# Tables in 128 rows of 1 KB, spread by TensorE into PSUM, in a rotary-embedding kernel

## Chip, cores and metric

The kernel runs on one core of a Trainium2 chip. The metric is the device time of one execution in microseconds (us), median of several executions. The profile's span, from the first instruction to the last, is 1.8 us shorter than that time in the kernel before. All runs compared here are in the fast state, except single executions on one core, whose state can't be told, and one slow execution in experiment 11; those are named.

## The reference

x is [8, 8, 1024, 64] in fp32, 16.8 MB, and so is the output; the two tables are [1024, 32], 131 KB each.

```python
x_first, x_second = x[..., :32], x[..., 32:]
out_first  = x_first * cos_cached - x_second * sin_cached
out_second = x_first * sin_cached + x_second * cos_cached
```

## The kernel before

x is cut into 8 units of 2 MB, [128 partitions, 64 positions, 64]. All units are loaded at once, one after another on SyncE's queue, and the stores follow on the same queue, each when its unit is ready.

The tables arrive as 32 rows of 4 KB on 32 partitions. Each of the 128 partitions needs 64 of the 1024 table rows, so TensorE spreads them (`sel` is a 0/1 matrix), and shuffles and copies bring the other half:

```python
rs, rc = sv[3][0:Q, 0:C], sv[3][0:Q, C:2 * C]            # Q = 32 partitions
nc.sync.dma_start(out=rs, in_=sin_cached.rearrange("(q n) j -> q (n j)", q=Q))
nc.scalar.dma_start(out=rc, in_=cos_cached.rearrange("(q n) j -> q (n j)", q=Q))
for m0, m1 in ((0, F // 2), (F // 2, F)):
    nc.sync.dma_start(out=xt[0][:, m0:m1], in_=xf[0][:, m0:m1])
for u in range(1, n_u):
    nc.sync.dma_start(out=xt[u], in_=xf[u])
# ... (cut)
for part, r in ((en[:, :BK], rs[:, :BK]), (en[:, BK:], rs[:, BK:]),
                (ec[0], rc[:, :BK]), (ec[1], rc[:, BK:])):
    nc.tensor.matmul(part, sel, r, start=True, stop=True)
odd = [2 * (i % (Q // 2)) + 1 for i in range(Q)]
for t, r in ((sn, rs), (cs, rc)):
    nc.vector.stream_shuffle(t[0:Q, H:], flat(r), odd)
nc.scalar.copy(out=tb4[Q:2 * Q, H:], in_=tb4[0:Q, H:])
for k in range(2, P // Q):
    nc.gpsimd.tensor_copy(out=tb4[k * Q:(k + 1) * Q, H:], in_=tb4[0:Q, H:])
# ... (cut) products of unit 0, then its sums on GpSimd
```

From unit 1 on, ScalarE stages x in PSUM, VectorE forms the four products, and GpSimd or TensorE sums them:

```python
for c, (u, n0, n1) in enumerate(chunks):
    (alone if (u, n0) in whole else products)(st[c], u, n0, n1)   # VectorE
    put(c + 2)                                                    # ScalarE stages a later chunk
    if c in back:
        pe_back(*back[c])                                         # ScalarE: TensorE's sums back
    if c in on_pe:
        pe_sums(*on_pe[c])                                        # TensorE
    for f, *args in behind.get(c, ()):
        f(*args)                                                  # GpSimd sums, stores
```

Of the kernel before, what the change touches and what calls it, by code (L numbers as in the profile page):

```python
# [8 lines left out]
def kernel(  # L9
# [7 lines left out]
    nc = tc.nc  # L17
    fp32 = mybir.dt.float32
    TT = mybir.AluOpType
    P = nc.NUM_PARTITIONS  # L20

    b, h, seq, hd = x.shape
    half = hd // 2
    R = 64
    F = R * hd
    T = R * half
    n_u = (b * h * seq) // (R * P)
    BK = 512
    G = BK // half
    Q = 32  # L30
    H = R // 2
    C = H * half
    assert seq == Q * H and n_u == 8 and R == 4 * G and H == 2 * G

    xf = x.rearrange("b h s d -> (b h s d)").rearrange(
        "(u p m) -> u p m", p=P, m=F)
# [4 lines left out]
    const = ctx.enter_context(tc.tile_pool(name="const", bufs=1))  # L41
# [3 lines left out]
    tb = const.tile([P, 2 * T], fp32, name="tb")  # L45
    tb4 = tb.rearrange("p (n t j) -> p n t j", t=2, j=half)
    plus = const.tile([P, P], fp32, name="plus")
    sel = const.tile([Q, P], fp32, name="sel")
    minus = const.tile([P, P], fp32, name="minus")


# [4 lines left out]
    def both(t):  # L56

        return t.rearrange("p (w n f) -> p n w f", w=2, f=hd)

    for i, (u0, u1) in enumerate(((3, 6), (0, 4), (1, 5))):  # L60
        w = xp.tile([P, 3 * F], fp32, name=f"w{i}")
        xt[u0], xt[u1] = w[:, :F], w[:, 2 * F:]
        sv[u0] = sv[u1] = w[:, F:2 * F]
        px[u0], px[u1] = both(w[:, :2 * F]), both(w[:, F:])[:, :, ::-1]
    K = 40
    L = R - K
    w = xp.tile([P, 2 * F + 2 * L * hd], fp32, name="w3")
    xt[2], xt[7] = w[:, :F], w[:, F + 2 * L * hd:]
    sv[2], sv[7] = w[:, (R - K) * hd:(R + L) * hd], w[:, F:F + 2 * L * hd]
    gt = w[:, F + L * hd:F + 2 * L * hd]  # L70
    px[2] = both(w[:, K * hd:(R + L) * hd])
    px[7] = both(w[:, F:F + 4 * L * hd])[:, :, ::-1]


    rs, rc = sv[3][0:Q, 0:C], sv[3][0:Q, C:2 * C]
    nc.sync.dma_start(out=rs, in_=sin_cached.rearrange("(q n) j -> q (n j)", q=Q))
    nc.scalar.dma_start(out=rc, in_=cos_cached.rearrange("(q n) j -> q (n j)", q=Q))


    for m0, m1 in ((0, F // 2), (F // 2, F)):  # L80
# [6 lines left out]
    for i in range(3):  # L87
        nc.sync.dma_start(out=row[:, i * hd:(i + 1) * hd], in_=xf[i][0:1, 0:hd])


    nc.gpsimd.memset(plus, 0.0)
    nc.gpsimd.affine_select(out=plus, in_=plus, compare_op=TT.not_equal, fill=1.0,
                            base=0, pattern=[[-1, P]], channel_multiplier=1)
    nc.scalar.copy(out=sel.rearrange("q (r j) -> q r j", j=Q // 2),
                   in_=plus[0:Q, 0:Q:2].unsqueeze(1).to_broadcast([Q, 2 * P // Q, Q // 2]))
    nc.scalar.mul(out=minus, in_=plus, mul=-1.0)

    cs, sn = tb4[:, :, 0], tb4[:, :, 1]

    def rows(t, n0, n1):  # L100
        return t[:, n0 * hd:n1 * hd].rearrange("p (n k j) -> p n k j", k=2, j=half)

    def tab(t, n0, n1):

        return t[:, n0:n1].unsqueeze(2).to_broadcast([P, n1 - n0, 2, half])

    def flat(t):
        return t.rearrange("p (n j) -> p n j", j=half)

    def mul(eng, o, a, t):  # L110
        eng.tensor_tensor(out=o, in0=a, in1=t, op=TT.mult)  # L111

    def sums(eng, o, c, s):
        eng.tensor_tensor(out=o[:, :, 0], in0=c[:, :, 0], in1=s[:, :, 1], op=TT.subtract)  # L114
        eng.tensor_tensor(out=o[:, :, 1], in0=c[:, :, 1], in1=s[:, :, 0], op=TT.add)  # L115

    def stage(pt, u, n0, n1):
        nc.scalar.copy(out=pt[:, :(n1 - n0) * hd], in_=xt[u][:, n0 * hd:n1 * hd])  # L118

    def products(pt, u, n0, n1):  # L120

        n = n1 - n0
        m = K if u == 2 else 0
        xr = pt[:, :n * hd].rearrange("p (n o f) -> p n o f", o=1, f=hd)
        tr = tb4[:, n0:n1].unsqueeze(3).to_broadcast([P, n, 2, 2, half])
        mul(nc.vector, px[u][:, n0 - m:n1 - m].rearrange("p n t (k j) -> p n t k j", k=2),
            xr.to_broadcast([P, n, 2, hd]).rearrange("p n t (k j) -> p n t k j", k=2), tr)

    def alone(pt, u, n0, n1):
        s = sv[4] if u == 7 else sv[u]  # L130
        xr, sr, pr = rows(xt[u], n0, n1), rows(s, n0, n1), rows(pt, 0, n1 - n0)
        mul(nc.vector, sr, pr, tab(sn, n0, n1))
        mul(nc.vector, pr, pr, tab(cs, n0, n1))
        sums(nc.vector, xr, pr, sr)

    def on_pool(u, n0, n1):
        xr, gr = rows(xt[u], n0, n1), rows(gt, 0, n1 - n0)
        mul(nc.gpsimd, gr, xr, tab(sn, n0, n1))
        mul(nc.gpsimd, xr, xr, tab(cs, n0, n1))
        sums(nc.gpsimd, xr, xr, gr)  # L140

    def pool_sums(u, n0, n1, c=None):
        xr = rows(xt[u], n0, n1)
        sums(nc.gpsimd, xr, rows(xt[u] if c is None else c, n0, n1), rows(sv[u], n0, n1))

    def store(u, n0=0, n1=R):
        nc.sync.dma_start(out=of[u][:, n0 * hd:n1 * hd], in_=xt[u][:, n0 * hd:n1 * hd])




    PS = bass.MemoryType.PSUM
    with ExitStack() as first:
        p0, p1 = [first.enter_context(tc.tile_pool(name=n, bufs=1, space=PS))
                  for n in ("p0", "p1")]
        en = p0.tile([P, C], fp32, name="en")
        ec = [p0.tile([P, BK], fp32, name=f"ec{i}") for i in range(2)]
        pre = p1.tile([P, 4 * BK], fp32, name="pre")
        for part, r in ((en[:, :BK], rs[:, :BK]), (en[:, BK:], rs[:, BK:]),
                        (ec[0], rc[:, :BK]), (ec[1], rc[:, BK:])):  # L160
            nc.tensor.matmul(part, sel, r, start=True, stop=True)  # L161
        odd = [2 * (i % (Q // 2)) + 1 for i in range(Q)]
        for t, r in ((sn, rs), (cs, rc)):
            nc.vector.stream_shuffle(t[0:Q, H:], flat(r), odd)  # L164
        nc.scalar.copy(out=tb4[Q:2 * Q, H:], in_=tb4[0:Q, H:])  # L165
        for k in range(2, P // Q):
            nc.gpsimd.tensor_copy(out=tb4[k * Q:(k + 1) * Q, H:], in_=tb4[0:Q, H:])  # L167
        mul(nc.vector, rows(sv[0], 0, H), rows(xt[0], 0, H), tab(flat(en), 0, H))
        for i in range(2):
            mul(nc.vector, rows(sv[7], i * G, (i + 1) * G), rows(xt[0], i * G, (i + 1) * G),  # L170
                tab(flat(ec[i]), 0, G))
        pool_sums(0, 0, H, sv[7])
        stage(pre, 0, H, R)
        nc.scalar.copy(out=sn[:, :H], in_=flat(en))
        for i in range(2):
            nc.scalar.copy(out=cs[:, i * G:(i + 1) * G], in_=flat(ec[i]))
        products(pre, 0, H, R)
        pool_sums(0, H, R)

    q0, q1, q2 = [ctx.enter_context(tc.tile_pool(name=n, bufs=1, space=PS))  # L180
                  for n in ("q0", "q1", "q2")]
    st, acc = {}, {}

    def pe_sums(u, n0):
        acc[u, n0] = q2.tile([P, 2 * BK], fp32, name="acc")
        a = acc[u, n0].rearrange("p (k n j) -> p k n j", k=2, j=half)
        xr, sr = rows(xt[u], n0, n0 + G), rows(sv[u], n0, n0 + G)
        for k in range(2):
            nc.tensor.matmul(a[:, k], plus, xr[:, :, k], start=True, stop=False)  # L189
            nc.tensor.matmul(a[:, k], plus if k else minus, sr[:, :, 1 - k],  # L190
                             start=False, stop=True)

    def pe_back(u, n0):
        a = acc[u, n0].rearrange("p (k n j) -> p n k j", k=2, j=half)
        nc.scalar.copy(out=rows(xt[u], n0, n0 + G), in_=a)  # L195

    on_pool(2, 0, K // 2)


    cuts = ((0, 24), (24, 48), (48, 64))  # L200
    chunks = [(u, n0, n1) for u in (1, 3, 4, 5, 6, 7) for n0, n1 in cuts]
    chunks.insert(3, (2, K, R))
    whole = {(7, 48)}
    on_pe = {0: (1, 0), 2: (1, 16), 4: (3, 0), 5: (3, 16), 7: (4, 0), 8: (4, 16),
             10: (5, 0), 13: (6, 0), 14: (6, 16)}
    back = {2: (1, 0), 3: (1, 16), 5: (3, 0), 6: (3, 16), 8: (4, 0), 10: (4, 16),
            12: (5, 0), 14: (6, 0), 15: (6, 16)}
    behind = {
        2: [(pool_sums, 1, 32, 64), (on_pool, 2, K // 2, K)],
        3: [(store, 1), (pool_sums, 2, K, 64), (store, 2)],  # L210
        6: [(pool_sums, 3, 32, 64), (store, 3)],
        9: [(pool_sums, 4, 32, 64)],
# [1 line left out]
        12: [(pool_sums, 5, 16, 64), (store, 5)],  # L214
        15: [(pool_sums, 6, 32, 64), (store, 6)],
        16: [(pool_sums, 7, 0, 24)],
        17: [(store, 7, 0, 24), (pool_sums, 7, 24, 48), (store, 7, 24, 48)],
        18: [(store, 7, 48, 64)],
    }

    def put(c):
        if c < len(chunks):
            u, n0, n1 = chunks[c]
            st[c] = (q1 if c % 2 else q0).tile([P, 3 * BK], fp32, name="st")
            stage(st[c], u, n0, n1)

    put(0)
    put(1)
    store(0)
    for c, (u, n0, n1) in enumerate(chunks):  # L230
        (alone if (u, n0) in whole else products)(st[c], u, n0, n1)
        put(c + 2)
        if c in back:
            pe_back(*back[c])
        if c in on_pe:
            pe_sums(*on_pe[c])
        for f, *args in behind.get(c, ()):
            f(*args)
# [29 lines left out]
```

## Time and profile before

| | before |
|---|---|
| time, median | 85.1 us (85.05 to 85.17) |
| span in the profile | 83.3 us |
| bytes moved | 33.82 MB |
| DMA rate, 6 to 80 us | 428 to 431 GB/s |
| GpSimd, VectorE busy | 80%, 82% |
| first and last load landed (units 0 and 7) | 9.2, 43.4 us |

The prediction below shows the lines. A line of the windows gives the stretch and its length, the busy us (and count of instructions) of TensorE, its weight loads, VectorE, ScalarE and GpSimd, TensorE's granted clock, and the DMA.

### The profile page before, as it was taken

The page shows a single profiled execution, that of the slowest core. Times are in us where ns is not written, and L with a number is a line of the kernel's source. Part 1 is how long each engine was busy: PE and PEld are TensorE (multiplying, and loading weights), DVE is VectorE, ACT ScalarE, POOL GpSimd, SP SyncE. Part 2 cuts the span into 40 slices and gives each one's busy share as a digit, 9 for nine tenths or more (in the row PEclk, how much of TensorE's full clock was granted, in tenths as well). Part 3 has the DMA queues.
Part 4 walks back from the last instruction along what each step waited for, and adds up shares of the span by engine and source line. Part 5 has one row for each costly group of instructions (what it writes and reads, how often), then busy time and mean ns, then how long its engine had stood idle before and what let it go on. Part 6 is the DMA issues. An engine that isn't in the chain of part 4 may idle for free.

```text
span 83.3 us, 389 instructions
## 1 busy us (share of the span) xinstructions
PE 44.3 (53%) x80; PEld 16.8 (20%) x80; DVE 68.5 (82%) x30; ACT 40.8 (49%) x36; POOL 67.1 (80%) x36
## 2 busy tenths in 40 slices
PE   0099940002995594958959495880996890000000
PEld 0043300002340241404224140420431420000000
DVE  0093999999999999999999999999999998960000
ACT  4408695463166557298096757666446708000000
POOL 3008909999999999999999999999999999993000
PEclk9999999999999999999999999999659999855555
DMA  2999999999999999999999999999999999999992
GB/s 43 236 437 429 421 448 433 448 417 393 448 433 448 425 386 448 433 448 425 393 441 433 448 425 425 441 401 448 425 456 425 409 456 393 456 425 395 425 415 102
DMA packets 2838, 33.82 MB, mean 406 GB/s; under 512 B 342, under 2 KB 342, under 8 KB 790
## 3 DMA queue, kind: packets, MB, share of 16 engines
q1 hardware_dynamic: 2790, 33.69, 96.2%
q10 hardware_dynamic: 48, 0.13, 0.5%
HBM read 17.04 MB, written 16.78 MB: 406 GB/s over the span
## 4 chain that ended last, share of the span: by engine, by line
POOL 64%; issue 13%; PE 5%; DMA 4%; DVE 3%; POOLq 2%
POOL w L115 26%; POOL w L114 24%; POOL w L111 14%; PE en L161 5%; DMA w<-in_sin_cached_dram 4%; DVE w L111 3%; POOLq L263 2%; POOLq L114 0%; POOLq L111 0%
## 5 line engine op out<-in xcount | busy, mean ns | idle before, releaser
L111 DVE TENSOR_TENSOR w<-st,tb 128x3072 f32<-128x3072 f32 (+2 forms) x19 | 54.7, 2957 | 0.3 <-ACT st L118 0.3
L118 ACT COPY st<-w 128x1536 f32<-128x1536 f32 (+1 forms) x19 | 24.9, 1310 | 15.7 <-DVE w L111 14.8
L189 PE MATMUL acc<-w,plus 128*128 128x512 f32 x36 | 21.5, 682 | 20.2 <-ACT w L195 11.2
L114 POOL TENSOR_TENSOR w<-w 128x1024 f32<-128x1024 f32 (+3 forms) x11 | 23.9, 2173 | 0.2
L115 POOL TENSOR_TENSOR w<-w 128x1024 f32<-128x1024 f32 (+3 forms) x11 | 23.9, 2169 | 0.0
L189 PEld LDWEIGHTS acc<-w,plus 128*128 128x128 f32 x36 | 6.9, 212 | 33.7 <-ACT w L195 17.8
L195 ACT COPY w<-acc 128x1024 f32<-128x1024 f32 x9 | 9.1, 1010 | 8.5 <-PE acc L190 8.5
L111 POOL TENSOR_TENSOR w<-w,tb 128x1280 f32<-128x1280 f32 x4 | 11.6, 2902 | 0.2
L190 PE MATMUL acc<-w,minus 128*128 128x512 f32 x18 | 11.0, 696 | 0.0
L190 PE MATMUL acc<-w,plus 128*128 128x512 f32 x18 | 9.2, 592 | 0.0
L167 POOL COPY tb<-tb 32x2048 f32<-32x2048 f32 x2 | 3.8, 1885 | 5.4 <-DVE tb L164 5.4
L161 PE MATMUL en<-w,sel 32*128 32x512 f32 x4 | 3.7, 1089 | 4.1 <-DMA w<-in_sin_cached_dram 4.1
L190 PEld LDWEIGHTS acc<-w,minus 128*128 128x128 f32 x18 | 4.0, 223 | 5.3 <-issue 5.3
L111 DVE TENSOR_TENSOR w<-pre,tb 128x4096 f32<-128x4096 f32 x1 | 4.4, 4419 | 0.0
L190 PEld LDWEIGHTS acc<-w,plus 128*128 128x128 f32 x18 | 3.4, 190 | 4.7 <-issue 4.7
L114 POOL TENSOR_TENSOR w<-w,w 128x1024 f32<-128x1024 f32 x1 | 2.3, 2338 | 2.2 <-issue 2.2
L165 ACT COPY tb<-tb 32x2048 f32<-32x2048 f32 x1 | 1.9, 1897 | 3.6 <-DVE tb L164 3.6
L161 PE MATMUL ec<-w,sel 32*128 32x512 f32 x4 | 3.6, 1056 | 0.0
L111 DVE TENSOR_TENSOR w<-w,en 128x2048 f32<-128x2048 f32 x1 | 2.3, 2287 | 1.4 <-PE en L161 1.4
L164 DVE LOAD_MASK_SELECT tb<-w x2 | 0.0, 8 | 4.0 <-DMA w<-in_sin_cached_dram 4.0
L164 DVE STREAM_SHUFFLE tb<-w 32x1024 f32<-32x1024 f32 x2 | 2.5, 1280 | 0.0
L111 DVE TENSOR_TENSOR w<-w,ec 128x1024 f32<-128x1024 f32 x2 | 2.4, 1218 | 0.0
(18 smaller groups left out, 14.2 us busy)
## 6 DMA issues: line engine op xcount, KB each, us to landing
w<-in_x_dram SPq DMA_DIRECT2D x7, 2048.0 KB, 29.3
out_dram<-w SPq DMA_DIRECT2D x7, 2048.0 KB, 10.5
w<-in_x_dram SPq DMA_DIRECT2D x2, 1024.0 KB, 5.5
out_dram<-w SPq DMA_DIRECT2D x2, 768.0 KB, 5.6
out_dram<-w SPq DMA_DIRECT2D x1, 512.0 KB, 6.4
w<-in_cos_cached_dram ACTq DMA_DIRECT2D x1, 128.0 KB, 3.6
w<-in_sin_cached_dram SPq DMA_DIRECT2D x1, 128.0 KB, 3.3
row<-in_x_dram SPq DMA_DIRECT2D x3, 0.2 KB
```

The costliest lines, as they stand in the source:

```text
L111: eng.tensor_tensor(out=o, in0=a, in1=t, op=TT.mult)
L114: eng.tensor_tensor(out=o[:, :, 0], in0=c[:, :, 0], in1=s[:, :, 1], op=TT.subtract)
L115: eng.tensor_tensor(out=o[:, :, 1], in0=c[:, :, 1], in1=s[:, :, 0], op=TT.add)
L118: nc.scalar.copy(out=pt[:, :(n1 - n0) * hd], in_=xt[u][:, n0 * hd:n1 * hd])
L161: nc.tensor.matmul(part, sel, r, start=True, stop=True)
L164: nc.vector.stream_shuffle(t[0:Q, H:], flat(r), odd)
L165: nc.scalar.copy(out=tb4[Q:2 * Q, H:], in_=tb4[0:Q, H:])
L167: nc.gpsimd.tensor_copy(out=tb4[k * Q:(k + 1) * Q, H:], in_=tb4[0:Q, H:])
L189: nc.tensor.matmul(a[:, k], plus, xr[:, :, k], start=True, stop=False)
L190: nc.tensor.matmul(a[:, k], plus if k else minus, sr[:, :, 1 - k], start=False, stop=True)
L195: nc.scalar.copy(out=rows(xt[u], n0, n0 + G), in_=a)
L263: with _tile.TileContext(nc) as tc:
```

## The change

The intent is a cheaper start. The tables come as 128 rows of 1 KB over all partitions. TensorE spreads them with a 128-row selector, 8 matmuls, behind one more matmul on constants, put there to get its clock up. VectorE reads the spread tables in PSUM for unit 0 while ScalarE copies them to SBUF for the others. The shuffles and the 32-partition copies go. GpSimd does 8 rows of unit 0 whole, takes 16 rows of unit 1 from TensorE, and gives 8 rows of unit 7 to VectorE.

```diff
-    rs, rc = sv[3][0:Q, 0:C], sv[3][0:Q, C:2 * C]
-    nc.sync.dma_start(out=rs, in_=sin_cached.rearrange("(q n) j -> q (n j)", q=Q))
-    nc.scalar.dma_start(out=rc, in_=cos_cached.rearrange("(q n) j -> q (n j)", q=Q))
+    raw = sv[3][:, :BK]
+    for eng, i, t in ((nc.sync, 0, sin_cached), (nc.scalar, 1, cos_cached)):
+        eng.dma_start(out=raw[:, i * BK // 2:(i + 1) * BK // 2],
+                      in_=t.rearrange("(q n) j -> q (n j)", q=P))
 ... (cut: selector made by VectorE; the old spreading, shuffles and copies removed)
-    on_pe = {0: (1, 0), 2: (1, 16), 4: (3, 0), ...
+    on_pe = {0: (1, 0), 4: (3, 0), ...
-        2: [(pool_sums, 1, 32, 64), (on_pool, 2, K // 2, K)],
+        2: [(pool_sums, 1, 16, 64), (on_pool, 2, K // 2, K)],
 ... (cut: unit 7 in 24, 16 and 24 rows in place of 24, 24 and 16)
+    nc.tensor.matmul(tp[6][:, :BK], plus, plus.unsqueeze(1).to_broadcast([P, BK // P, P]),
+                     start=True, stop=True)
+    rt = raw.rearrange("q (t n j) -> q n t j", t=2, j=half)
+    for b, t in tp.items():
+        for k in range(t.shape[1] // BK):
+            nc.tensor.matmul(t[:, k * BK:(k + 1) * BK], sel[:, (b + k) * P:(b + k + 1) * P], rt,
+                             start=True, stop=True)
... (cut: the helpers first and keep)
+    keep(0, 1)
+    on_pool(0, 0, B)
+    first(1, 1)
+    keep(1, 1)
+    first(2, 2)
 ... (cut: and so on for blocks 4 and 6)
```

More of the change, by code (lines that the diff above doesn't have):

```diff
@@ L29 @@
     G = BK // half
-    Q = 32
+    B = seq // P
+    N = R // B
+    S = P // N
     H = R // 2
-    C = H * half
-    assert seq == Q * H and n_u == 8 and R == 4 * G and H == 2 * G
+    assert n_u == 8 and R == 4 * G and B * hd == BK and S * R == seq
     xf = x.rearrange("b h s d -> (b h s d)").rearrange(
@@ L47 @@
     plus = const.tile([P, P], fp32, name="plus")
-    sel = const.tile([Q, P], fp32, name="sel")
     minus = const.tile([P, P], fp32, name="minus")
@@ L58, in both @@
         return t.rearrange("p (w n f) -> p n w f", w=2, f=hd)
-    for i, (u0, u1) in enumerate(((3, 6), (0, 4), (1, 5))):
+    for i, (u0, u1) in enumerate(((3, 6), (4, 0), (1, 5))):
         w = xp.tile([P, 3 * F], fp32, name=f"w{i}")
@@ L63 @@
         sv[u0] = sv[u1] = w[:, F:2 * F]
-        px[u0], px[u1] = both(w[:, :2 * F]), both(w[:, F:])[:, :, ::-1]
+        px[u0], px[u1] = both(w[:, :2 * F])[:, :, ::-1], both(w[:, F:])
     K = 40
@@ L70 @@
     gt = w[:, F + L * hd:F + 2 * L * hd]
-    px[2] = both(w[:, K * hd:(R + L) * hd])
-    px[7] = both(w[:, F:F + 4 * L * hd])[:, :, ::-1]
-    rs, rc = sv[3][0:Q, 0:C], sv[3][0:Q, C:2 * C]
-    nc.sync.dma_start(out=rs, in_=sin_cached.rearrange("(q n) j -> q (n j)", q=Q))
-    nc.scalar.dma_start(out=rc, in_=cos_cached.rearrange("(q n) j -> q (n j)", q=Q))
+    px[2] = both(w[:, K * hd:(R + L) * hd])[:, :, ::-1]
+    px[7] = both(w[:, F:F + 4 * L * hd])
+    raw = sv[3][:, :BK]
+    for eng, i, t in ((nc.sync, 0, sin_cached), (nc.scalar, 1, cos_cached)):
+        eng.dma_start(out=raw[:, i * BK // 2:(i + 1) * BK // 2],
+                      in_=t.rearrange("(q n) j -> q (n j)", q=P))
     for m0, m1 in ((0, F // 2), (F // 2, F)):
@@ L88 @@
         nc.sync.dma_start(out=row[:, i * hd:(i + 1) * hd], in_=xf[i][0:1, 0:hd])
+    sel = sv[3][:, BK:BK + N * P]
     nc.gpsimd.memset(plus, 0.0)
@@ L93 @@
                             base=0, pattern=[[-1, P]], channel_multiplier=1)
-    nc.scalar.copy(out=sel.rearrange("q (r j) -> q r j", j=Q // 2),
-                   in_=plus[0:Q, 0:Q:2].unsqueeze(1).to_broadcast([Q, 2 * P // Q, Q // 2]))
+    nc.vector.tensor_copy(
+        out=sel.rearrange("q (k r j) -> q k r j", k=N, j=S),
+        in_=plus.rearrange("q (j k) -> q k j", k=N).unsqueeze(2).to_broadcast([P, N, N, S]))
     nc.scalar.mul(out=minus, in_=plus, mul=-1.0)
-    cs, sn = tb4[:, :, 0], tb4[:, :, 1]
+    sn, cs = tb4[:, :, 0], tb4[:, :, 1]
     def rows(t, n0, n1):
@@ L105, in tab @@
         return t[:, n0:n1].unsqueeze(2).to_broadcast([P, n1 - n0, 2, half])
-    def flat(t):
-        return t.rearrange("p (n j) -> p n j", j=half)
     def mul(eng, o, a, t):
@@ L118, in stage, with products @@
         nc.scalar.copy(out=pt[:, :(n1 - n0) * hd], in_=xt[u][:, n0 * hd:n1 * hd])
-    def products(pt, u, n0, n1):
+    def products(xr, u, n0, n1, t):
         n = n1 - n0
         m = K if u == 2 else 0
-        xr = pt[:, :n * hd].rearrange("p (n o f) -> p n o f", o=1, f=hd)
-        tr = tb4[:, n0:n1].unsqueeze(3).to_broadcast([P, n, 2, 2, half])
         mul(nc.vector, px[u][:, n0 - m:n1 - m].rearrange("p n t (k j) -> p n t k j", k=2),
-            xr.to_broadcast([P, n, 2, hd]).rearrange("p n t (k j) -> p n t k j", k=2), tr)
+            xr.rearrange("p (n o f) -> p n o f", o=1, f=hd).to_broadcast([P, n, 2, hd])
+            .rearrange("p n t (k j) -> p n t k j", k=2),
+            t.unsqueeze(3).to_broadcast([P, n, 2, 2, half]))
     def alone(pt, u, n0, n1):
@@ L140, in on_pool, with pool_sums @@
         sums(nc.gpsimd, xr, xr, gr)
-    def pool_sums(u, n0, n1, c=None):
+    def pool_sums(u, n0, n1):
         xr = rows(xt[u], n0, n1)
-        sums(nc.gpsimd, xr, rows(xt[u] if c is None else c, n0, n1), rows(sv[u], n0, n1))
+        sums(nc.gpsimd, xr, xr, rows(sv[u], n0, n1))
     def store(u, n0=0, n1=R):
         nc.sync.dma_start(out=of[u][:, n0 * hd:n1 * hd], in_=xt[u][:, n0 * hd:n1 * hd])
+    st, acc, q = {}, {}, []
     PS = bass.MemoryType.PSUM
-    with ExitStack() as first:
-        p0, p1 = [first.enter_context(tc.tile_pool(name=n, bufs=1, space=PS))
-                  for n in ("p0", "p1")]
-        en = p0.tile([P, C], fp32, name="en")
-        ec = [p0.tile([P, BK], fp32, name=f"ec{i}") for i in range(2)]
-        pre = p1.tile([P, 4 * BK], fp32, name="pre")
-        for part, r in ((en[:, :BK], rs[:, :BK]), (en[:, BK:], rs[:, BK:]),
-                        (ec[0], rc[:, :BK]), (ec[1], rc[:, BK:])):
-            nc.tensor.matmul(part, sel, r, start=True, stop=True)
-        odd = [2 * (i % (Q // 2)) + 1 for i in range(Q)]
-        for t, r in ((sn, rs), (cs, rc)):
-            nc.vector.stream_shuffle(t[0:Q, H:], flat(r), odd)
-        nc.scalar.copy(out=tb4[Q:2 * Q, H:], in_=tb4[0:Q, H:])
-        for k in range(2, P // Q):
-            nc.gpsimd.tensor_copy(out=tb4[k * Q:(k + 1) * Q, H:], in_=tb4[0:Q, H:])
-        mul(nc.vector, rows(sv[0], 0, H), rows(xt[0], 0, H), tab(flat(en), 0, H))
-        for i in range(2):
-            mul(nc.vector, rows(sv[7], i * G, (i + 1) * G), rows(xt[0], i * G, (i + 1) * G),
-                tab(flat(ec[i]), 0, G))
-        pool_sums(0, 0, H, sv[7])
-        stage(pre, 0, H, R)
-        nc.scalar.copy(out=sn[:, :H], in_=flat(en))
-        for i in range(2):
-            nc.scalar.copy(out=cs[:, i * G:(i + 1) * G], in_=flat(ec[i]))
-        products(pre, 0, H, R)
-        pool_sums(0, H, R)
@@ L180, with pool @@
-    q0, q1, q2 = [ctx.enter_context(tc.tile_pool(name=n, bufs=1, space=PS))
-                  for n in ("q0", "q1", "q2")]
-    st, acc = {}, {}
+    def pool(c, name, side):
+        return c.enter_context(tc.tile_pool(name=name, bufs=1, space=PS, side=side,
+                                            reuse_waits="tile"))
     def pe_sums(u, n0):
-        acc[u, n0] = q2.tile([P, 2 * BK], fp32, name="acc")
+        acc[u, n0] = q[2].tile([P, 2 * BK], fp32, name="acc")
         a = acc[u, n0].rearrange("p (k n j) -> p k n j", k=2, j=half)
@@ L195, in pe_back @@
         nc.scalar.copy(out=rows(xt[u], n0, n0 + G), in_=a)
-    on_pool(2, 0, K // 2)
     cuts = ((0, 24), (24, 48), (48, 64))
-    chunks = [(u, n0, n1) for u in (1, 3, 4, 5, 6, 7) for n0, n1 in cuts]
+    last = ((0, 24), (24, 40), (40, 64))
+    chunks = [(u, n0, n1) for u in (1, 3, 4, 5, 6, 7) for n0, n1 in (last if u == 7 else cuts)]
     chunks.insert(3, (2, K, R))
-    whole = {(7, 48)}
-    on_pe = {0: (1, 0), 2: (1, 16), 4: (3, 0), 5: (3, 16), 7: (4, 0), 8: (4, 16),
+    whole = {(7, 40)}
+    on_pe = {0: (1, 0), 4: (3, 0), 5: (3, 16), 7: (4, 0), 8: (4, 16),
              10: (5, 0), 13: (6, 0), 14: (6, 16)}
-    back = {2: (1, 0), 3: (1, 16), 5: (3, 0), 6: (3, 16), 8: (4, 0), 10: (4, 16),
+    back = {2: (1, 0), 5: (3, 0), 6: (3, 16), 8: (4, 0), 10: (4, 16),
             12: (5, 0), 14: (6, 0), 15: (6, 16)}
     behind = {
-        2: [(pool_sums, 1, 32, 64), (on_pool, 2, K // 2, K)],
+        2: [(pool_sums, 1, 16, 64), (on_pool, 2, K // 2, K)],
         3: [(store, 1), (pool_sums, 2, K, 64), (store, 2)],
@@ L216 @@
         16: [(pool_sums, 7, 0, 24)],
-        17: [(store, 7, 0, 24), (pool_sums, 7, 24, 48), (store, 7, 24, 48)],
-        18: [(store, 7, 48, 64)],
+        17: [(store, 7, 0, 24), (pool_sums, 7, 24, 40), (store, 7, 24, 40)],
+        18: [(store, 7, 40, 64)],
     }
@@ L223, in put, with first, keep @@
             u, n0, n1 = chunks[c]
-            st[c] = (q1 if c % 2 else q0).tile([P, 3 * BK], fp32, name="st")
+            st[c] = q[c % 2].tile([P, 3 * BK], fp32, name="st")
             stage(st[c], u, n0, n1)
-    put(0)
+    one, two = ExitStack(), ctx.enter_context(ExitStack())
+    tp = {b: pool(c, f"t{b}", side).tile([P, n * BK], fp32, name="tab") for b, n, c, side in
+          ((0, 1, one, "right"), (1, 1, one, "right"), (2, 2, one, "right"),
+           (4, 2, two, "left"), (6, 2, two, "left"))}
+    nc.tensor.matmul(tp[6][:, :BK], plus, plus.unsqueeze(1).to_broadcast([P, BK // P, P]),
[5 more added lines that the diff above has]
+                             start=True, stop=True)
+    def first(b, n):
+        products(xt[0][:, b * BK:(b + n) * BK], 0, b * B, (b + n) * B,
+                 tp[b].rearrange("p (n t j) -> p n t j", t=2, j=half))
+    def keep(b, n):
+        nc.scalar.copy(out=tb[:, b * BK:(b + n) * BK], in_=tp[b])
+    keep(0, 1)
[3 more added lines that the diff above has]
+    first(2, 2)
+    keep(2, 2)
+    pool_sums(0, B, H)
+    first(4, 2)
+    keep(4, 2)
+    one.close()
+    q.append(pool(ctx, "q0", "right"))
+    put(0)
+    first(6, 2)
+    keep(6, 2)
+    pool_sums(0, H, R)
+    two.close()
+    q += [pool(ctx, "q1", "left"), pool(ctx, "q2", "left")]
     put(1)
+    on_pool(2, 0, K // 2)
     store(0)
     for c, (u, n0, n1) in enumerate(chunks):
-        (alone if (u, n0) in whole else products)(st[c], u, n0, n1)
+        if (u, n0) in whole:
+            alone(st[c], u, n0, n1)
+        else:
+            products(st[c][:, :(n1 - n0) * hd], u, n0, n1, tb4[:, n0:n1])
         put(c + 2)
```

## The prediction

The sum came to about -0.2 us, 84.9 us: two terms are cut from it, a gain at the start and a small cost of the smaller packets, so those that still stand, 0 and 0, don't add up to it.

> **What bounds the kernel now.** I read three views: the slices of the page, the DMA windows, and single stores in the timeline and the DMA list. The engine totals invite a wrong answer: VectorE is busy 82% and GpSimd 80%, and the chain that ended last is mostly GpSimd.
>
> ```profile
> PE 44.3 (53%) x80; PEld 16.8 (20%) x80; DVE 68.5 (82%) x30; ACT 40.8 (49%) x36; POOL 67.1 (80%) x36
> ...
> DVE  0093999999999999999999999999999998960000
> POOL 3008909999999999999999999999999999993000
> ...
> DMA  2999999999999999999999999999999999999992
> ...
> HBM read 17.04 MB, written 16.78 MB: 406 GB/s over the span
> ...
> POOL 64%; issue 13%; PE 5%; DMA 4%; DVE 3%; POOLq 2%
> ```
>
> The reader should compare the right-hand ends of the rows. The engines stop three or more slices (2.08 us each) before the end, and the DMA row doesn't: it is full from the second slice to the last but one. So the computing ends about 76 us and 6 us of transfers remain. The windows say how full "full" is:
>
> ```profile
> 0.00:2.00 2.00, 0.00 (x0) 0.00 (x0) 0.00 (x0) 0.83 (x1) 0.70 (x6) 1.00 0.22 37
> 2.00:4.00 2.00, 0.00 (x0) 0.00 (x0) 0.00 (x0) 0.96 (x3) 0.00 (x0) 1.00 0.98 254
> 4.00:6.00 2.00, 1.86 (x3) 0.85 (x4) 1.97 (x4) 0.00 (x0) 0.00 (x0) 1.00 0.95 393
> 6.00:42.00 36.00, 22.25 (x39) 8.18 (x37) 34.59 (x14) 21.07 (x18) 32.76 (x15) 1.00 1.01 431
> 42.00:80.00 38.00, 20.17 (x40) 7.78 (x40) 31.97 (x14) 17.96 (x16) 33.59 (x16) 0.86 1.00 428
> ...
> 82.00:83.30 1.30, 0.00 (x0) 0.00 (x0) 0.00 (x0) 0.00 (x0) 0.00 (x0) 0.50 0.00 0
> ```
>
> The last two columns are the busy share of the 16 DMA engines and GB/s. From 6 to 80 us the share is 1.0 at 428 to 431 GB/s, in the loading half as in the storing half. What's left of the span is a start (the first packet moves at 1.76 us by the trace's packet times, then the rate climbs), and an end of 1.3 us without bytes. Bytes at that rate are the bound: 33.82 MB / 0.4295 = 78.7 us, plus 1.76 and 1.3, makes 81.8 of 83.3; the other 1.5 us is slow start and drain.
>
> This holds only while a store is always waiting in the queue. The stores are issued by SyncE in order behind the loads:
>
> ```profile
> 23.92 53.05 SPq L147 DMA_DIRECT2D out_dram<-w  x10
> 69.72 0.33 SPq L147 DMA_DIRECT2D out_dram<-w  x1
> ...
> out_dram<-w SPq DMA_DIRECT2D x1, 2048.0 KB, 24.4
> ...
> out_dram<-w SPq DMA_DIRECT2D x1, 2048.0 KB, 10.5
> ...
> out_dram<-w SPq DMA_DIRECT2D x1, 512.0 KB, 6.4
> ```
>
> The first store is ready at 23.9 and lands 24.4 us later: the last load lands at 43.4 (packet times), and 4.9 us later this store. Unit 4's store takes 10.5 us, the last one, 0.5 MB, 6.4. They stand in a queue. Landings come every 4.85 us, so I can give each store its turn (when the store before it lands) and its spare time. Unit 4 is issued at 57.26 and lands at 67.7; unit 5 then at 72.6; unit 6 at 77.4. Unit 6 is issued at 69.72 for a turn at 72.6; less some 1.5 us (1.0 from an issue to its first packet, as at the start: 0.73 to 1.76; 0.5 from the last byte to the landing: 81.99 to 82.46) that is 1.4 us spare, the smallest of all. Unit 5 has 2.2, the second piece of unit 7 2.1, the rest 3 or more.
>
> [...]
>
> **The change part by part.**
>
> *Table loads.* Same bytes (2 x 131 KB). Now 128 rows of 1 KB: each DMA engine gets 16 packets of 1 KB for 4 of 4 KB. [...] How much can a better start give at all? Against 430 GB/s the stream lost (430-254) x 2 = 352 KB and (430-393) x 2 = 74 KB in the two windows, and 30 KB in the quarter of a microsecond before: 456 KB, 1.06 us. That caps the gain at 1.1 us, 1.2% of 85.1. [...]
>
> *Unit 0, before to after.* Removed: two stream shuffles (2 x 1.28 on VectorE), a 32-partition table copy on ScalarE (1.90) and two on GpSimd (3.81), staging of the upper half of x (1.87). Added: a selector copy on VectorE (1024 elements, about 1.2, before the tables arrive), 8 matmuls with 128 rows at 0.85, and four reads of tables from PSUM by VectorE as products (1024 outputs 1.22, then 3 x 2.29 = 8.1 us in all). Old VectorE work there: 2.29 + 2.43 + 4.42 = 9.1 plus the shuffles.
> VectorE after: x's first half lands at 6.66; 6.7 to 7.9; the fourth table block comes at about 8.1, so to 10.4; the second half of x is in at 9.2; to 12.7; to 15.0. The next product needs unit 1 (landed about 14.05) plus staging of 1.44: 15.5 us, for 16.81 before. VectorE is 1.3 us ahead.
> GpSimd after: it computes 8 rows of unit 0 whole, products 2 x 1.16 (512 of 1280 elements at 2.90), sums 2 x 0.63: 3.6, from 6.7 to 10.3; sums of 24 rows 2 x 1.82 = 3.6, to 14.0; waits for VectorE until 15.0; 32 rows 2 x 2.34, to 19.7. Store 0 then goes at 19.7 for 23.92: worth nothing, as its turn is at 43.4.
>
> *Moved.* GpSimd takes 16 rows of unit 1 from TensorE: sums of 48 rows (2 x 3.48) for 32 (2 x 2.36), +2.2 us. After on_pool for unit 2 (8.9 us, to 28.6) it ends unit 1 at 35.5; before, also 35.5. From there both GpSimd sequences are equal, so stores 2 to 6 are issued at the old times or slightly earlier (unit 6 waits for ScalarE's copy behind VectorE, which is 1.3 us ahead). Unit 7 shifts 8 rows from GpSimd (-1.2 us, it ends near 74.4) to VectorE alone, 24 rows 2 x 1.75 + 2 x 0.95 = 5.4 and a 2.28 product for 3.35 and 3.8: +0.5, ending near 73.6.
>
> *Sum on the path that sets the end.* [...]steady stream 0, end 0: about -0.2 us, 84.9 us. All computing that is saved becomes longer waiting of stores in the queue.
>
> **Rivals.**
> - *The engines are the bound, as the chain (GpSimd 64%) suggests.* Then about 1.2 us of an earlier finish would show, 83.9. Against it: the full DMA row and 6.4 us for a 0.5 MB store. Even then GpSimd gains only in the last unit.
> - *The start becomes much better or worse.* If all 1.06 us came back: 84.0. If [...]tables landed late: perhaps +0.5, 85.6.
> - *A new wait stalls the engines*: half-clock matmuls late by 2 us, [...]staging behind the table copies. Up to about 1.4 us of delay carried to unit 6 costs nothing; a 3 us delay would cost about 1.6, 86.7. Against it: the estimated lead of 1.3 us on VectorE.
>
> **Range and chances.** The bound's bytes don't change, and gain is capped at 1.1 us where 2% is 1.7. So faster by 2% gets 0.02. Slower needs over 3 us of lost computing: 0.04. Within 2%: 0.94. Range 84.4 to 85.5: a start 0.5 better or 0.4 worse than now.
>
> **What would show it.** Right: 428 to 431 GB/s again from 6 to 80 us, store 0 issued near 19.7 but landing near 48, first chunk of unit 1 near 15.5, end of computing 75 or earlier, span within 0.5 us of 83.3. The last load's landing, 43.4 before, tells what the start gave: I expect 43.2. Wrong: a slice of the DMA row below 9 in the second half (a store missed its turn), or a last load earlier by over 0.8 us.

What the trace of the kernel before shows: both tables land on 32 partitions, in 64 packets of 4 KB, of which five took 667 ns and half 159 to 161, and the window of 2 to 4 us has 254 GB/s. (Over 16 engines 64 packets are 4 for each on average; the changed kernel's trace has 256 of 1 KB, 16 for each.) By itself this doesn't tell the shape of the loads from a slow start as such. "Half-clock" refers to the weight loads of the 128-row matmuls, 0.85 us apart from 20.2 us and 0.43 from 24.7; those of the 32-row matmuls stayed 0.85 apart for all of their 7.2 us.

## The result and the profile after

The changed kernel takes 85.4 us (85.24 to 85.53, 4 runs), the kernel before beside it 85.07 (85.03 to 85.17). The ratio is 1.0036, interval 1.0017 to 1.0056. That is the same within 2%, as predicted, and inside the range. But the small difference is clear of noise and has the other sign: 0.3 us slower, not 0.2 faster.

The page of the changed kernel:

```profile
DVE  3105799899999999999796999999999995994000
POOL 3008979599999999999999999999999999990000
...
DMA  1999999999999999999989999999999999999992
GB/s 21 355 412 459 447 431 439 423 423 431 416 463 416 431 423 431 431 416 439 314 369 416 447 416 431 431 439 431 431 447 400 439 439 416 447 431 391 411 437 94
...
HBM read 17.04 MB, written 16.78 MB: 405 GB/s over the span
...
DVE 33%; PE 23%; issue 16%; ACT 12%; DMA 3%; ACTq 2%; DVEq 1%
```

The chain of waits has changed its name from GpSimd to VectorE, TensorE and ScalarE, and means as little as it did: the DMA row is full again. What's new is in the GB/s row. The second slice is up, and slices 20 and 21, at 40 to 44 us, stand at 314 and 369 in a row that is otherwise near 430. They aren't idle: the busy share is 8 to 9 tenths. The transfers there are slow, not absent.

Where the tables land (the DMA issues, before and then after; the last number is us from issue to landing):

```profile
w<-in_cos_cached_dram ACTq DMA_DIRECT2D x1, 128.0 KB, 3.6
w<-in_sin_cached_dram SPq DMA_DIRECT2D x1, 128.0 KB, 3.3
```

```profile
w<-in_cos_cached_dram ACTq DMA_DIRECT2D x1, 128.0 KB, 2.7
w<-in_sin_cached_dram SPq DMA_DIRECT2D x1, 128.0 KB, 2.6
```

So the tables are 0.7 to 0.9 us earlier. The windows of the changed kernel, against those in the prediction:

```profile
2.00:4.00 2.00, 1.87 (x3) 0.47 (x2) 0.43 (x1) 0.75 (x2) 0.00 (x0) 1.00 1.02 340
40.00:42.50 2.50, 2.50 (x7) 0.92 (x5) 2.10 (x1) 0.29 (x1) 2.42 (x2) 1.00 0.96 275
42.00:80.00 38.00, 19.17 (x42) 7.19 (x40) 32.22 (x14) 18.22 (x16) 33.01 (x16) 0.89 1.00 426
80.00:83.60 3.60, 0.00 (x0) 0.00 (x0) 0.00 (x0) 0.00 (x0) 0.00 (x0) 0.50 0.57 237
```

and of the kernel before, the one window of these that the prediction doesn't have:

```profile
40.00:42.50 2.50, 1.58 (x4) 0.38 (x2) 2.50 (x2) 0.88 (x1) 2.42 (x2) 1.00 0.98 419
```

From 2 to 4 us the stream moves 340 instead of 254 GB/s; from 40 to 42.5 us it moves 275 instead of 419. The second costs (419 - 275) x 2.5 = 360 KB, 0.84 us at 430 GB/s. The landings in the trace agree: the loads of units 3 to 6 land 0.33 to 0.34 us earlier than before (unit 3 at 23.49 for 23.83), the last one 0.30 us later (43.72 for 43.42), and from there every store lands 0.3 us or slightly more later (unit 4's at 68.10 for 67.75).

In the packets themselves: a 16 KB packet takes 612 ns. In this stretch 37 of them took over 640 ns, up to 1349. I use two measures below, both worked out from the trace's packet records (a third follows in the account of the prediction). The *loss* is the time over 612 ns of all 16 KB packets over 640 ns between 30 and 50 us, divided by 16 engines: 0.79 us here, 0.00 before. The *largest gap* tells whether the engines run in step: of the 16 packet starts in one round of 0.615 us, taken at 20 us, the largest distance between neighbours. Before, it was 0.24 us (two bunches of starts); after, 0.17 (scattered).

So there is one small gain and one larger loss in the same stream, and two questions: what makes the loss, and was the engines' work really without influence?

### The profile page after: what moved, and what is told of

Read it like the earlier page. It is cut to its first block, busy times and chain, and to the rows that moved or that the text cites. A ratio compares the mean times of both kernels' runs of the same rounds, so it can differ in the third digit from the quotient of the medians.

```text
span 83.6 us, 387 instructions
## 1 busy us (share of the span) xinstructions
PE 45.5 (54%) x82; PEld 17.6 (21%) x82; DVE 66.9 (80%) x27; ACT 37.8 (45%) x34; POOL 67.3 (81%) x38
## 4 chain that ended last, share of the span: by engine, by line
DVE 33%; PE 23%; issue 16%; ACT 12%; DMA 3%; ACTq 2%; DVEq 1%
DVE w L112 30%; PE acc L163 9%; ACT st L119 8%; PE acc L164 8%; PE tab L212 6%; ACT w L169 4%; DMA w<-in_cos_cached_dram 3%; DVE st L112 2%; ACTq L278 2%; DVE w L115 1%; DVEq L278 1%; ACT tb L220 1%; DVEq L112 0%
## 5 line engine op out<-in xcount | busy, mean ns | idle before, releaser
L163 PE MATMUL acc<-w,plus 128*128 128x512 f32 x32 | 20.4, 724 | 21.4 <-ACT w L169 8.3
L115 POOL TENSOR_TENSOR w<-w 128x1024 f32<-128x1024 f32 (+4 forms) x12 | 26.1, 2176 | 1.7 <-DVE w L112 1.4
L116 POOL TENSOR_TENSOR w<-w 128x1024 f32<-128x1024 f32 (+4 forms) x12 | 26.1, 2175 | 0.0
L112 POOL TENSOR_TENSOR w<-w,tb 128x1280 f32<-128x1280 f32 (+1 forms) x6 | 14.2, 2368 | 5.4 <-DMA w<-in_x_dram 5.2
L112 DVE TENSOR_TENSOR w<-w,tab 128x2048 f32<-128x2048 f32 (+1 forms) x4 | 7.9, 2018 | 5.1 <-PE tab L212 5.1
L212 PE MATMUL tab<-w 128*128 128x512 f32 x16 | 8.6, 700 | 0.1
L164 PE MATMUL acc<-w,plus 128*128 128x512 f32 x16 | 8.6, 625 | 0.0
L220 ACT COPY tb<-tab 128x1024 f32<-128x1024 f32 (+1 forms) x5 | 4.2, 843 | 8.4 <-DVE w L112 5.5
L212 PEld LDWEIGHTS tab<-w 128*128 128x128 f32 x16 | 3.6, 233 | 5.9 <-issue 5.9
L207 PE MATMUL tab<-plus 128*128 128x512 f32 x2 | 2.1, 1141 | 1.4 <-POOL plus L95 1.4
L112 DVE TENSOR_TENSOR st<-st,tb 128x1536 f32<-128x1536 f32 x1 | 1.8, 1756 | 0.0
L115 DVE TENSOR_TENSOR w<-st,w 128x768 f32<-128x768 f32 x1 | 1.0, 958 | 0.0
L116 DVE TENSOR_TENSOR w<-st,w 128x768 f32<-128x768 f32 x1 | 0.9, 947 | 0.0
```

The lines of the kernel that those rows point to most:

```text
L112: eng.tensor_tensor(out=o, in0=a, in1=t, op=TT.mult)
L115: eng.tensor_tensor(out=o[:, :, 0], in0=c[:, :, 0], in1=s[:, :, 1], op=TT.subtract)
L116: eng.tensor_tensor(out=o[:, :, 1], in0=c[:, :, 1], in1=s[:, :, 0], op=TT.add)
L163: nc.tensor.matmul(a[:, k], plus, xr[:, :, k], start=True, stop=False)
L164: nc.tensor.matmul(a[:, k], plus if k else minus, sr[:, :, 1 - k], start=False, stop=True)
L207: nc.tensor.matmul(tp[6][:, :BK], plus, plus.unsqueeze(1).to_broadcast([P, BK // P, P]), start=True, stop=True)
```

## The experiments

The kernel before took 85.05, 85.03 and 85.16 us (medians) on three chips; every kernel is compared with the kernel before on the same chip.

**1 and 2. Both kernels again.** No edit. They ask if the slow stretch belongs to the program or fell into one execution by chance.

> The changed kernel once more, as it is. In its first profile the loads of units 3 to 6 landed 0.33 us earlier than before, but the last load 0.30 us later: between 40.1 and 42.5 us 38 load packets of 16 KB took up to 1349 ns instead of 612. Theory A (the dip belongs to this program): the dip is there again, at about 40 us, the span is 83.5 to 83.7 and the time about 85.4. Theory B (a chance event of the memory): the dip is gone or elsewhere, and a run without it has a span of about 83.0 and 84.75 us.

> The kernel before once more. Theory A: again no slow packets (at most 1 of the 16 KB packets over 640 ns), last load landed at 43.4 us, 85.1 us. Theory B: a dip of about 0.6 us in some executions, at any place, 85.1 to 85.7 us.

The changed kernel: 85.44 us (85.33 to 86.46), ratio 1.0067, interval 1.0006 to 1.0127. The slow packets are there again from 40.1 us on, loss 0.76. Its profiled run was the slowest one, span 84.7; there unit 3 landed at 23.89. One engine was late by itself: it ended the last load at 44.50, the other fifteen by 43.48, and the last load landed 1.08 us later than in the changed kernel's first trace, as much as the span is longer. The kernel before, one run of unknown state: 85.39 us, span 83.6, with a loss of 0.30 us at 40.3 to 41.3 us. So neither theory holds as put: the stretch exists in both programs at the same place, and it is mild or absent before and large after.

> The kernel before a third time, for its trace. Theory C (32-row tables leave the DMA engines in step, and engines in step lose little at the end of the loads): the largest gap between packet starts in a round at 20 us is 0.24 us or more, the loss of the packets over 640 ns at 40 to 42.5 us is at most 0.3 us, span 83.2 to 83.6. A gap under 0.2 us, or a loss of 0.5 us or more, would speak against it.

85.08 us, loss 0.24, largest gap 0.40. The kernel before thus has losses of 0.00, 0.30 and 0.24 with largest gaps of 0.24, 0.42 and 0.40.

**3. The old buffer addresses.** The removed selector shifted all large buffers by 512 bytes per partition; an unused tile shifts them back.

```diff
     plus = const.tile([P, P], fp32, name="plus")
+    pad = const.tile([32, P], fp32, name="pad")
     minus = const.tile([P, P], fp32, name="minus")
```

> The changed kernel with an unused 512-byte tile put where the selector stood, so that all the large buffers have their old SBUF addresses again. If the dip comes from where the last load is written in SBUF (addresses 512 bytes lower than before), it goes: span 83.0, 84.75 us. If the addresses don't matter: as the changed kernel, 85.4 us with the dip at 40 us.

85.55 us (85.16 to 85.76), ratio 1.0048, loss 0.75 where the changed kernel had 0.79 and 0.76. The addresses made no difference.

**4. The changed kernel with the old shape of table loads.** 32 rows of 4 KB; the result is wrong.

```diff
... (cut: raw and sel moved so that nothing overlaps)
+    for p0, p1 in ((32, 64), (64, P)):
+        nc.gpsimd.memset(sv[3][p0:p1, BK // 2 * 3:BK // 2 * 5], 0.0)
     for eng, i, t in ((nc.sync, 0, sin_cached), (nc.scalar, 1, cos_cached)):
-        eng.dma_start(out=raw[:, i * BK // 2:(i + 1) * BK // 2],
-                      in_=t.rearrange("(q n) j -> q (n j)", q=P))
+        eng.dma_start(out=sv[3][0:32, i * 2 * BK:(i + 1) * 2 * BK],
+                      in_=t.rearrange("(q n) j -> q (n j)", q=32))
```

> The changed kernel with its tables loaded as before, as 32 rows of 4 KB (the result is wrong on purpose; instructions, waits and the bytes of the tables are the same, save for two small memsets). If the start's gain is the spread over all partitions, the sin table lands at 4.0 instead of 3.3 us and the loads of units 3 to 6 land 0.33 us later again (unit 3's at 23.8): 85.7 us if the dip stays, 85.1 if it doesn't. If the gain came from elsewhere: 23.5 us and 85.4 us.

The tables land at 3.85 and 4.20 us again, and the slow stretch is gone, though all the rest is the changed kernel, save the two memsets and the place of the buffers:

```profile
2.00:4.00 2.00, 1.50 (x2) 0.50 (x2) 1.09 (x1) 0.77 (x2) 0.37 (x2) 1.00 1.06 285
40.00:42.50 2.50, 2.50 (x6) 0.76 (x4) 2.28 (x1) 0.11 (x1) 2.42 (x2) 1.00 0.99 419
```

Loss 0.01, largest gap 0.34, last load at 43.25. The spans of its four runs are 83.2 to 83.6, those of the kernel before 83.2 to 83.6. The time, however, is 85.41 us, ratio 1.0037: here 1.9 to 2.1 us lie outside the span, for 1.8 elsewhere. The same holds of experiments 5, 7 and 8 (1.9 to 2.1 us), which like this one have added GpSimd instructions; why is open. For these four I therefore give spans too. Unit 3's load landed at 23.68, between the first traces of the two kernels, where 23.8 was expected.

**5. The kernel before with the new shape of table loads**, the other way round; again wrong.

```diff
-    rs, rc = sv[3][0:Q, 0:C], sv[3][0:Q, C:2 * C]
-    nc.sync.dma_start(out=rs, in_=sin_cached.rearrange("(q n) j -> q (n j)", q=Q))
-    nc.scalar.dma_start(out=rc, in_=cos_cached.rearrange("(q n) j -> q (n j)", q=Q))
+    rs = rc = sv[3][0:Q, 0:C]
+    for eng, i, t in ((nc.sync, 0, sin_cached), (nc.scalar, 1, cos_cached)):
+        eng.dma_start(out=sv[3][:, i * BK // 2:(i + 1) * BK // 2],
+                      in_=t.rearrange("(q n) j -> q (n j)", q=P))
+    nc.gpsimd.memset(sv[3][0:Q, BK:C], 0.0)
```

> The kernel before with only the loads of its tables changed to 128 rows of 1 KB (wrong result on purpose: the same 32 partitions are then read). Theory C (the shape of the table loads does both things: it starts the stream 0.33 us earlier, and leaves the 16 DMA engines out of step, which the last load pays for at 40 to 42.5 us): unit 3's load lands at 23.5 instead of 23.8, the largest gap between packet starts in a round of 0.62 us falls from 0.24 us or more to 0.20 or less, packets over 900 ns appear at 40 to 42.5 us, span 83.4 to 83.8, time 85.2 to 85.6 us. Theory D (the dip comes from something else in the changed kernel): no dip, span 83.0, 84.75 us.

85.47 us (85.16 to 86.16), ratio 1.0042, interval 1.0007 to 1.0078; spans 83.2 to 84.2, median 83.6, for 83.2 to 83.8, median 83.4, of the kernel before. Nothing but the shape of 262 KB of loads and one small memset is new, and this kernel has the better start and the slow stretch:

```profile
2.00:4.00 2.00, 0.40 (x1) 0.43 (x2) 0.38 (x2) 0.95 (x3) 0.00 (x0) 1.00 0.99 342
40.00:42.50 2.50, 1.40 (x4) 0.49 (x3) 2.50 (x2) 1.42 (x2) 2.42 (x3) 1.00 1.02 315
```

Loss 0.73, largest gap 0.16, unit 3 at 23.54, last load at 43.56: as theory C said. Experiments 4 and 5, one trace each, together put the slow stretch on the shape of the table loads, whichever kernel they stand in. The shape is two things at once, 64 packets of 4 KB to 32 partitions or 256 of 1 KB to 128; no run separates them.

**6. No computing after unit 0.** Each store waits for its unit's load alone; wrong.

```diff
-    on_pool(2, 0, K // 2)
     store(0)
-    for c, (u, n0, n1) in enumerate(chunks):
-        ... (products, staging, sums)
+    for c in range(len(chunks)):
+        for f, *args in behind.get(c, ()):
+            if f is store:
+                f(*args)
```

> The changed kernel with all computing after unit 0 left out (wrong result on purpose): each store waits only for its unit's load. The DMA work is the same. If the stream alone sets the end, as predicted, the time doesn't fall by more than the loss at 40 us: 84.7 to 85.4 us. If the engines were the bound: far less than 84. On the dip: if it comes from what the engines do at 40 us, it is gone (span 83.0); if from the transfers themselves, 83.5 or more with packets over 900 ns at 40 to 42.5 us.

85.35 us (85.14 to 85.99), ratio 1.0059. GpSimd goes from 67.3 us busy to 12.8, VectorE from 66.9 to 9.0, and the time stays. The windows:

```profile
6.00:40.00 34.00, 5.37 (x13) 2.09 (x11) 7.90 (x4) 6.44 (x6) 12.09 (x8) 0.63 1.02 433
40.00:42.50 2.50, 0.00 (x0) 0.00 (x0) 0.00 (x0) 0.00 (x0) 0.00 (x0) 0.50 0.96 328
45.00:80.00 35.00, 0.00 (x0) 0.00 (x0) 0.00 (x0) 0.00 (x0) 0.00 (x0) 0.50 1.00 428
```

The reader should see two things. The rates are those of the working kernel, so the stream alone sets the end. And the middle line has no instruction on any engine, and still 328 GB/s: the slow stretch is made by the transfers, not by engines that get in their way.

**7 and 8. Later GpSimd.** Useless sums ahead of those of unit 4, about 1.45 and 4.7 us.

```diff
+    def spare(n):
+        gr = rows(gt, 0, n)
+        sums(nc.gpsimd, gr, gr, gr)
-        9: [(pool_sums, 4, 32, 64)],
+        9: [(spare, 8), (pool_sums, 4, 32, 64)],                 # the other: spare 20, spare 12
```

> The changed kernel with 1.45 us of useless GpSimd work (two sums of 8 rows) ahead of the sums of unit 4. By the queue argument unit 6's store has some 1.9 us to spare here (issued at 69.5, last bytes of unit 5 at 72.5, less 1.0 from issue to packets), so 0 to 0.1 us of change: 85.4 us. If GpSimd were the bound: +1.45, 86.9 us.

> The same with 32 rows, about 4.7 us. Unit 6's store would be issued at 74.2 and its packets start at 75.2, in place of 72.5: the DMA row empties for about 2.7 us and the time grows by 2.7 to 2.8, to 88.2 us. If GpSimd were the bound: +4.7, 90.1 us; if computing never mattered: 85.4 us.

With 1.45 us the spans are 83.3 to 84.0, median 83.6, like the changed kernel's (its first runs had 83.5 to 83.7); the time is 85.64 us, ratio 1.0064, of which some 0.2 us is outside the span as in experiment 4. The window of 60 to 70 us shows share 1.01 at 433 GB/s: no gap. With 4.7 us (one run, state unknown) it is 87.95 us, span 85.9, 2.3 us above 83.6; 2.7 was expected. Its windows show the queue running dry:

```profile
58.00:62.00 4.00, 3.67 (x8) 1.44 (x8) 4.00 (x2) 1.75 (x2) 4.00 (x3) 1.00 1.01 434
62.00:66.00 4.00, 2.31 (x6) 1.12 (x7) 4.00 (x2) 2.55 (x3) 4.00 (x3) 1.00 0.83 352
66.00:70.00 4.00, 1.39 (x4) 0.32 (x2) 2.99 (x3) 2.36 (x2) 4.00 (x2) 0.97 0.57 242
```

Here share falls with the rate, which is how waiting for a store looks, and not as at 40 us, where the share stays near 1 and the rate falls. Computing has about 2 us to spare (4.7 added, 2.3 paid, in this one run), and what goes beyond that shows in the time.

**9. Another last load.** Units 6 and 7 change places in the queue.

```diff
-    for u in range(1, n_u):
+    for u in (1, 2, 3, 4, 5, 7, 6):
```

> The changed kernel with the loads of units 6 and 7 in the other order. The last load is then unit 6, into another buffer, from another part of x. If the dip belongs to unit 7's data or buffer it moves to some 35 to 38 us; if it belongs to the last load or to the moment it stays at 40 to 42.5 us. Time 85.4 us either way, unless unit 6's load coming 4.9 us later than now (43.7 for 38.2) holds up nothing: it isn't needed before about 57 us.

85.23 us (85.07 to 85.25), ratio 1.0015. The slow packets stay at 40.1 to 42.3 us, loss 0.48, with another buffer and other data.

**10. The last load behind the first store.**

```diff
-    for u in range(1, n_u):
+    for u in range(1, n_u - 1):
         nc.sync.dma_start(out=xt[u], in_=xf[u])
     ...
     store(0)
+    nc.sync.dma_start(out=xt[7], in_=xf[7])
```

> The changed kernel with the last load (unit 7) issued behind the first store instead of ahead of it. The queue then holds loads to about 38.2 us, store 0 to 43, unit 7's load to 48. If the slow packets are tied to the time, they show at 40 to 42.5 in the store; if to the last load's second half, at about 45 to 47.5; if to the loads just ahead of the first store, at about 35.5 to 38. If they need reads at that time alone, the dip is gone: span 83.0, 84.75 us, faster than both kernels.

85.6 us (85.38 to 86.45), ratio 1.0066, interval 1.0030 to 1.0102. The windows:

```profile
35.00:37.50 2.50, 2.13 (x4) 0.58 (x2) 2.50 (x2) 0.78 (x2) 2.50 (x2) 0.77 1.10 354
40.00:42.50 2.50, 1.93 (x5) 0.57 (x3) 2.50 (x1) 0.53 (x1) 2.42 (x2) 1.00 0.99 426
44.50:47.00 2.50, 2.23 (x6) 0.69 (x4) 2.50 (x2) 1.00 (x2) 2.50 (x2) 1.00 1.01 380
```

The stretch at 40 us is gone, and two others have come, 35.3 to 37.5 and 44.8 to 47.2 us: each time the last 2.5 us or so of loads ahead of a store. So it is tied to no moment and no data, but to the turn of the queue from loads to stores; two turns lose 1.01 us. The second and third of the expected places were both right; I had taken them for alternatives.

**11. Both tables on ScalarE's queue**, an attempt to keep the better start with other packets in front.

```diff
-    for eng, i, t in ((nc.sync, 0, sin_cached), (nc.scalar, 1, cos_cached)):
+    for eng, i, t in ((nc.scalar, 0, sin_cached), (nc.scalar, 1, cos_cached)):
```

> The changed kernel with both table loads issued by ScalarE, so that x leads SyncE's queue and the tables' packets come in turn with it. The bytes are the same, so the stream gains little: 0 to -0.2 us at the start, tables landing up to 0.5 us later. If the DMA engines stay out of step and theory C holds, the dip stays and the time is 85.2 to 85.5; if x's large packets ahead bring them into step, it goes and the time is 84.7.

A clear miss: 89.9 us (89.28 to 90.45, five runs; a sixth, 91.03, was slow), ratio 1.0555. The list of waits says why:

```profile
PE tab L212 <- DMA w<-in_cos_cached_dram: 6.0, 1, 6.0
```

TensorE starts on the tables at 9.43 us in place of 3.56. In the trace the tables' 256 packets of 1 KB, 46 ns each, are spread from 2.5 to 8.6 us among x packets of 8 KB, 309 ns each. Everything is 5.9 us later, the spare time of about 2 us is used up, and between 40 and 55 us the DMA share is 0.82 at 346 GB/s. The loss at the turn was 0.21 us here with a largest gap of 0.17, so by this measure the engines were scattered and didn't pay the usual price. (A third measure, below, removes this exception.)

## Why the prediction was right and where it was wrong

The time came out inside the range partly by luck: the start gave more than forecast, and a loss that the forecast didn't have took it away again.

- **The bound.** Right. With four fifths of the computing gone the time stayed (experiment 6), and the stream ran at 433 GB/s from 6 to 35 us, where all 13 traces besides experiment 11 have 429 to 433. Lateness is free up to some 2 us and counts beyond (7 and 8). Predicted spare time at unit 6's store was 1.4 us before; the changed kernel issues it at 69.54 instead of 69.72.
- **Table loads, the gain at the start.** Right in kind, and rather too small for a sum of -0.2. The tables themselves land 0.7 us or more earlier (4.0 to 3.3 us for sin), and the first packet moves at 1.76 us in either shape. The landing of unit 3's load seems to say that x hardly gained: 23.83, 23.60 and 23.53 in three traces of the kernel before, and 23.49 to 23.89, mean 23.60, in nine traces with 1 KB rows on both queues. But a landing is set by the last of the 16 engines. In the packet records 16 packets of 4 bytes close each load, one for each engine as it seems, and unit 3's load lands 0.43 to 0.50 us after the last of them in every trace. The average engine is done with unit 3 at 22.95 to 23.20, mean 23.07, in the four traces with 4 KB rows and at 22.63 to 22.82, mean 22.73, in the nine: 0.34 us won, of which the last engine shows 0.07 (23.21 to 23.14). The first 10 us of both kernels, with 4 KB rows (before, after_32) and with 1 KB rows (before_128, after), agree in the last column:

```profile
0.00:10.00 10.00, 5.86 (x7) 2.49 (x8) 4.55 (x5) 4.49 (x5) 4.00 (x8) 1.00 0.85 315
0.00:10.00 10.00, 7.50 (x13) 3.06 (x14) 3.40 (x3) 2.76 (x4) 4.58 (x11) 1.00 0.83 315
0.00:10.00 10.00, 6.40 (x8) 2.49 (x8) 5.11 (x6) 4.82 (x5) 4.86 (x9) 1.00 0.85 334
0.00:10.00 10.00, 8.51 (x14) 3.46 (x15) 3.53 (x3) 2.77 (x4) 4.08 (x10) 1.00 0.84 333
```

  All four 4 KB traces have 315 to 318 GB/s there, all nine 1 KB traces 326 to 334.
- **"Steady stream 0".** This is the term that failed. Of the 13 traces besides experiment 11, those with 4 KB table rows lose 0.00 to 0.30 us around the turn from loads to stores (393 to 419 GB/s from 40 to 42.5 us), the nine with 1 KB rows 0.47 to 1.01. In the eight of these without experiment 10 (275 to 367 GB/s from 40 to 42.5 us) the average engine, 0.34 us ahead at unit 3, ends the last load 0.18 us behind the 4 KB traces (42.98 for 42.80): the stretch cost it 0.52 us. The last engine, which sets the time, ends it 0.37 us later (43.45 for 43.08; 0.22 without the one late engine of experiment 1), for a measured 0.33. The rival "the start becomes much better or worse" came nearest in size, +0.5, but put it at the wrong end of the loads.
- **Small packets, the cost.** No such cost can be seen while they moved: the table packets' times add up to 0.90 to 1.14 us per engine with 4 KB rows and to 0.86 to 1.05 with 1 KB rows. What the new shape left behind cost more.
- **VectorE and GpSimd in unit 0.** Sizes right: unit 1 starts at 15.70 us for 15.5, GpSimd ends unit 0 at 20.2 for 19.7. Store 0 was to go at 19.7 and went at 23.58. I had overlooked a line of SyncE's waits in the kernel before, 

```profile
SPq L147 <- DMA w<-in_x_dram: 4.7, 1, 4.7
```

  and took 23.92 for the end of GpSimd's work. The store went 0.09 us after unit 3's load had landed, in both kernels (23.83 and 23.92; 23.49 and 23.58). Why it waits for another unit's load isn't shown; a semaphore that both share would be a guess. As said in the prediction, it's worth nothing.
- **End of computing.** Expected at 75 us or earlier; it is 76.2. VectorE lost 2.8 us waiting for staging, as ScalarE waited for TensorE's sums; the clock records of the changed kernel show TensorE at half clock (0.50 granted) from 16.9 to 23.7 and 27.1 to 37.3 us. It was hidden by the queue.
- **The last load at 43.2.** It was 43.7. I had named it as the sign for the start; it showed the turn instead, and the last engine instead of all.

What stays open is how the loss at the turn comes about. Shown are: the shape of the table loads decides it (4 and 5), computing isn't needed for it (6), it goes with the turn (10), and largest gaps of 0.24 us or more went with losses of at most 0.30, those of 0.20 or less with 0.47 or more, experiment 11 apart. The third measure, how far apart the 16 engines end unit 3's load, orders all 14 traces: 0.2 to 0.44 us with losses of at most 0.30 (experiment 11 is the 0.44), 0.50 to 1.02 with 0.47 or more. One rival can be struck out from the records: wherever there are slow packets, the first starts 1.8 us or more before any engine is done with the last load ahead of the store, so no engine had come to the store yet. That the engines' being out of step is the cause is not shown; no run changed it by itself, and none tells the packets' size from the partitions that they go to. No version was found that beats both kernels.

## What to carry to other kernels

Where the transfers are the bound, as here, removing work from the engines only makes stores wait longer (85.35 us with GpSimd busy for 12.8 us instead of 67.3); look for the DMA row, not the chain, and work out each store's spare time. A change in a small early transfer can alter how the DMA engines run much later (here 262 KB of tables at the start, and 275 to 367 instead of 393 to 419 GB/s from 40 to 42.5 us, experiments 10 and 11 apart), so follow the rate through every stretch, and take three traces of either kernel before explaining tenths of a microsecond. A landing tells of the last engine only (unit 3's: 0.07 us won, where the average engine won 0.34); count the bytes by a given time as well. With 1 KB table rows each turn of the queue from loads to stores cost about half a microsecond here, so load in one piece and store in one piece.
